# Weight splits and rotations of a decoder layer's front: from VectorE and GpSimd together to VectorE alone

## The chip, the cores and the metric

The kernel runs on one core of one Trainium2 chip. A core has TensorE (matrix products, into PSUM), VectorE, ScalarE and GpSimd (element-wise work), SyncE, which here issues the DMAs, and 16 DMA engines between HBM and SBUF. Each engine works through its own queue in order, and the engines wait for one another on semaphores. The metric is the device time of one execution in microseconds; lower is better.

## The reference

One decoder layer on 256 tokens of width 1024, all in float32. Two attention branches run in parallel on the normed input and are merged through sigmoid gates; a feed-forward part with 32 experts, of which each token uses four, follows; a gated per-layer embedding closes the layer. Cut to what matters here:

```python
proj = rmsnorm(x, g_mix) @ w_in          # q_a, k_a, v_a, c_q, c_kv, k_pe, gate_a, gate_b
q_a = apply_rope(rmsnorm(heads_a(q_a), moba_q_norm))
k_a = apply_rope(rmsnorm(heads_a(k_a), moba_k_norm))
y_a = moba_attention(q_a, k_a, heads_a(v_a))             # 8 heads of 64
q_b = rmsnorm(c_q, mla_q_lat_norm) @ w_uq                # 8 heads of 64 + 32
kv  = rmsnorm(c_kv, mla_kv_lat_norm) @ w_ukv             # k_nope, v_b
k_b = rmsnorm(concat([k_nope, k_pe shared by all heads]), mla_k_norm)
q_b, k_b: apply_rope on the last 32 of 96
y_b = causal_attention(q_b, k_b, v_b)
x = x + (sigmoid(gate_a) * (y_a @ w_branch_a) + sigmoid(gate_b) * (y_b @ w_branch_b)) @ w_out
x = x + routed_experts(rmsnorm(x, g_ffn), ...)           # 32 experts, top 4, clamped SwiGLU
x = x + sigmoid(rmsnorm(x, g_ple) @ w_ple_gate) * (p @ w_ple_proj)
```

`apply_rope` rotates pairs of halves: `[x1*cos - x2*sin, x2*cos + x1*sin]`.

## The kernel before

The program has two parts. The **front**, up to about 212 us, does everything up to the router; the **experts** then stream all 32 experts' weights (2 MB slots, six for each expert) through ten slots of SBUF, four of gate and up weights and two of down weights for each expert. SyncE issues every load in one fixed order (`seq`, `release`); a load is put in the queue where the slot's last reader is programmed, and waits there until that reader is done. Most of the ten slots are used by the front first: for the split weights and activations (`fcr`, `fbr`, `far`), for scratch (`scr0`, `scr1`), for the raw weights (`raw`, later `raw_o`), for the gates. So the front's end hands over most of the ten slots.

**Weight units and their split.** The front's weights are 51 units (lists `KINDS`, `UNITS`): those of the latents, q, k and v projections (four each), sixteen gate units of eight k-tiles by 128 columns, three for the latent up-projections, eight branch units (b) and eight output units (o). Each unit is at most 128x1024 in float32. The products are done in three passes of a reduced format (`three`, L260 to L262): an activation and a weight are each split into a high part, rounded to that format, and a low part, the rest, and high*high, high*low and low*high are summed. `make_unit` makes the two parts: ScalarE casts the unit into `hi` (L216), then `lo = src - hi` (L220) is done by VectorE on the first five eighths of the columns and by GpSimd on the rest; for the o units by VectorE alone. `unit` keeps at most `AHEAD = 3` units made ahead of the one that TensorE uses, in three or four split buffers: the cast of a unit waits until TensorE is done with the unit three before. `fetch` issues the load of a raw unit when the raw buffer's earlier unit has been split.

**Norm and rotation.** `rope_tables` multiplies the norm gains into the cosines and sines (GpSimd, L342 to L356), once for each of four gain vectors (`CA`, `WA` for the first branch, `CB`, `WB` for the second). `moba_norm(i)` squares and sums q or k for the norm, multiplies the swapped halves by `WA` (L412, into `t3`), the straight ones by `CA` (L414, VectorE, into `t5`), adds both (L416, VectorE), and for k scales (L418). The norm of q goes into the softmax's scale. `mla_stats` and `mla_norm` do the same for the second branch: the swapped halves of the 32 rotated columns times `WB` (L521, into `rt2`), the rest by VectorE (L523, L524), and the keys' gain (L526), then scaled per head (L528, L529). The shared key part `kpe` is rotated once (L509 to L512). `rsqrt` is a chain of small VectorE operations (L88 to L97); ScalarE scales the latents with its result (L434, L435).

**Order.** The program is written in the order of the source and scheduled when it is built: a list scheduler sets the order of each engine's queue from an estimate of when operands are there, so operations may stand far from their place in the source. `tc.issue_after(x)` holds the instructions in its block that run on x's engine behind x in that engine's queue; instructions of other engines are not held by it. The rotation tables are so held behind GpSimd's last split made up to there (`last_split[1]`), `x_stats` behind VectorE's (`last_split[0]`), and `mla_norm` behind a masking operation of VectorE (`masked[1]`).

The attention runs in eight rounds (`for j in range(8)`), one pair of heads each: scores on TensorE (L564, L566), masking and maximum on VectorE (L575, L579), exponentials on ScalarE (L581), reciprocal and scaling on VectorE (L583, L585), transposes of the probabilities on TensorE (L594), copies on ScalarE (L596), values on TensorE (L606, L607). Gate units are put between these steps to keep TensorE at work.

Of the kernel before, what the change touches and what calls it, by code (L numbers as in the profile page):

```python
# [27 lines left out]
ALU = mybir.AluOpType  # L28
# [22 lines left out]
UNITS = [(kind, n) for kind, c, n in KINDS for _ in range(c)]  # L51
# [3 lines left out]
FIRST_O = len(UNITS) - 8  # L55
# [10 lines left out]
def hybrid_layer(ctx, tc, x, p, b_down, w_ple_gate, w_ple_proj, bgu3, xt, tabs, wpre, wgu, wdn, out):  # L66
    nc = tc.nc
    V, A, G, T = nc.vector, nc.scalar, nc.gpsimd, nc.tensor
# [138 lines left out]
            load(t, wpre[:, U_OFF[n]:U_OFF[n + 1]])  # L207
            sent_units[0] += 1

    taken, raw_o, last_split = {}, [], [None, None]  # L210

    def make_unit(n):
        src = raw_of(n)[1]
        taken[split_of(n)] = n
        hi, lo = (split[split_of(n)][:, u, 0:UNITS[n][1]] for u in range(2))
        A.copy(hi, src)  # L216
        c = UNITS[n][1] * 5 // 8 if n < FIRST_O else UNITS[n][1]
        for e, a, b in ((V, 0, c), (G, c, UNITS[n][1])):
            if b > a:
                o = e.tensor_tensor(lo[:, a:b], src[:, a:b], hi[:, a:b], op=ALU.subtract)  # L220
                last_split[int(a > 0)] = o.ins

    def unit(k):
        n = used[0]
# [151 lines left out]
    project(512, lambda tt, b: A.mul(qk[:, tt, 0:512], b, xrs[0][:, tt:tt + 1]), x_stats)  # L376
    xrs = xrs[0]

    with tc.issue_after(last_split[1]):
        rope_tables()  # L380


    rbw = wk.tile([P, 2, P], F32, name="rbw")
# [3 lines left out]
    b = bank("rbc")  # L387
# [11 lines left out]
    def moba_norm(i):  # L399
        src, t3, t5 = ([t.rearrange("p (h d) -> p h d", h=8) for t in v] for v in (  # L400
            [qk[:, tt, i * 512:(i + 1) * 512] for tt in range(2)], [sq[:, tt * 512:(tt + 1) * 512] for tt in range(2)],
            [lat[:, tt, 512:1024] for tt in range(2)]))
        for tt in range(2):
            A.square(t3[tt], src[tt])
            V.tensor_reduce(hssb[:, i, tt], t3[tt], axis=AX.X, op=ALU.add)
        if i:
            hrs = rsqrt(wk, hssb.rearrange("p i a b -> p (i a b)"), 32, 64, "ha").rearrange("p (i t h) -> p i t h", i=2, t=2)
            V.tensor_scalar_mul(hrs[:, 0], hrs[:, 0], 64.0 ** -0.5)
            qscale[0], hrs = hrs[:, 0], hrs[:, 1]
        for tt in range(2):  # L410
            for u in range(2):
                G.tensor_tensor(t3[tt][:, :, u * 32:u * 32 + 32], src[tt][:, :, 32 - u * 32:64 - u * 32],  # L412
                                WA[i][:, tt:tt + 1, u * 32:u * 32 + 32].broadcast_to([P, 8, 32]), op=ALU.mult)
            V.tensor_tensor(t5[tt], src[tt], CA[i][:, tt:tt + 1].broadcast_to([P, 8, 64]), op=ALU.mult)  # L414
        for tt in range(2):
            V.tensor_tensor(src[tt], t5[tt], t3[tt], op=ALU.add)  # L416
            if i:
                V.tensor_tensor(src[tt], src[tt], hrs[:, tt].unsqueeze(2).broadcast_to([P, 8, 64]), op=ALU.mult)  # L418
# [21 lines left out]
    for tt in range(2):  # L440
        b = bank("latT")
        for i in range(3):
            T.transpose(b[:, i * P:(i + 1) * P], lsq[:, tt, i * P:(i + 1) * P], ident)
        for i in range(3):
            c = slice(i * P, (i + 1) * P)
# [7 lines left out]
    for c0, c1 in ((0, 512), (512, 768)):  # L453
        wh, wl = unit(2)
        for tt in range(2):
            b = bank("uq")
# [5 lines left out]
    for c0 in (0, 512):  # L462
        for tt in range(2):
            b = bank("ukv")
# [25 lines left out]
    q4 = qb[:, :, 0:768].rearrange("p t (h d) -> p t h d", h=8)  # L490
    kf4 = kbf[:, :, 0:768].rearrange("p t (h d) -> p t h d", h=8)
# [22 lines left out]
    def mla_norm():  # L514
# [3 lines left out]
        brs[0] = r  # L518
        for tt in range(2):
            for u in range(2):  # L520
                G.tensor_tensor(rt2[:, :, u * 16:u * 16 + 16], q4[:, tt, :, 80 - u * 16:96 - u * 16],  # L521
                                WB[0][:, tt:tt + 1, u * 16:u * 16 + 16].broadcast_to([P, 8, 16]), op=ALU.mult)
            V.tensor_tensor(q4[:, tt], q4[:, tt], CB[0][:, tt:tt + 1].broadcast_to([P, 8, 96]), op=ALU.mult)  # L523
            V.tensor_tensor(q4[:, tt, :, 64:96], q4[:, tt, :, 64:96], rt2, op=ALU.add)  # L524
            kr = brs[0][:, tt, 8:16].unsqueeze(2)
            G.tensor_tensor(kf4[:, tt, :, 0:64], kv4[:, tt, :, 0:64],  # L526
                            CB[1][:, tt:tt + 1, 0:64].broadcast_to([P, 8, 64]), op=ALU.mult)
            V.tensor_tensor(kf4[:, tt, :, 0:64], kf4[:, tt, :, 0:64], kr.broadcast_to([P, 8, 64]), op=ALU.mult)  # L528
            V.tensor_tensor(kf4[:, tt, :, 64:96], kpr[:, tt, 0:1].broadcast_to([P, 8, 32]),  # L529
# [112 lines left out]
    for ft in range(8):  # L642
        wh, wl = unit(8)
        bs = []
        for i in range(2):
            b = bank("br")
# [511 lines left out]
```

## Time and profile before

| | |
|---|---|
| runs | 1154.72, 1156.03, 1156.2 us; median 1156.03 |
| profiled execution | 1153.93 us, span 1151.9 us |
| busy over the span | TensorE 1077.9 us (94%), VectorE 328.4 (29%), ScalarE 209.5 (18%), GpSimd 79.0 (7%, 82 instructions, all in the front) |
| DMA | 440.15 MB, mean 382 GB/s |

The span is the time from the first to the last instruction of one profiled execution. Engines appear as PE (TensorE), DVE (VectorE), ACT (ScalarE), POOL (GpSimd) and SP or SPq (SyncE and its DMA queue); L220 is line 220 of the kernel. The share of busy time is a mean over stages with different limits, so it does not tell by itself what sets the end. A wait is shown with what ended it, as `[2.78 <-DVE fr L220]`: 2.78 us without work, ended by VectorE's write of tile `fr` at L220. The tile `fr` holds split parts, `lat` and `pre` hold parts of the norms and rotations, `w_g` and `w_d` expert weights.

### The profile page before, as it was taken

How to read it: one execution, taken by the hardware profiler on the slowest of the kernel's cores; microseconds unless marked ns; L12 is line 12 of the kernel's file. 1: busy time of each engine (PE TensorE's matmuls, PEld its weight loads, DVE VectorE, ACT ScalarE, POOL GpSimd, SP SyncE). 2: the span in 40 equal slices, each digit the busy share in tenths (PEclk: the TensorE clock that was granted, in tenths of full speed). 3: DMA queues.
4: the chain of work that ended last, by engine and by line, in shares of the span. 5: the costliest groups of instructions: out<-in, count | busy, mean ns of one | idle time of the engine just before them, and what ended most of it. 6: DMA issues, size and time to landing. Idle time of an engine off the chain costs nothing. (4 is left out here: it accounts for less than half of the span.)

```text
span 1151.9 us, 13101 instructions
## 1 busy us (share of the span) xinstructions
PE 1077.9 (94%) x5446; PEld 524.7 (46%) x5446; DVE 328.4 (29%) x730; ACT 209.5 (18%) x393; POOL 79.0 (7%) x82
## 2 busy tenths in 40 slices
PE   9799999999999999998889999998998989898988
PEld 7688997543434343342333434343433333333336
DVE  5679688321111121111110111120111111111136
ACT  5576753110000000000001000000000000000024
POOL 5752320000000000000000000000000000000000
PEclk9999999999999999999999999998999999999999
DMA  9544569999999999999999999999999999999991
GB/s 369 189 146 147 183 201 356 374 428 431 432 429 432 430 430 431 431 428 414 430 431 431 429 432 430 430 431 427 431 431 432 427 431 431 430 431 431 428 387 42
DMA packets 40079, 440.15 MB, mean 382 GB/s; under 512 B 4432, under 2 KB 5200, under 8 KB 14832
## 3 DMA queue, kind: packets, MB, share of 16 engines
q1 hardware_dynamic: 40016, 439.27, 91.3%
q8 instruction: 44, 0.72, 0.2%
q14 instruction: 19, 0.16, 0.0%
HBM read 438.21 MB, written 1.05 MB: 381 GB/s over the span
## 5 line engine op out<-in xcount | busy, mean ns | idle before, releaser
L861 PE MATMUL g<-w_g,xg 128*64 128x512 f32 x1024 | 294.5, 600 | 22.0 <-DMA w_g<-in_wgu 17.4
L861 PE MATMUL u<-w_g,xg 128*64 128x512 f32 x1024 | 290.9, 595 | 0.0
L885 PE MATMUL y<-w_d,ht 128*64 128x512 f32 x992 | 227.0, 597 | 11.9 <-DMA w_d<-in_wdn 11.9
L861 PEld LDWEIGHTS g<-w_g,xg 128*64 128x64 f32 x1024 | 78.7, 137 | 167.2 <-issue 122.6
L865 DVE TENSOR_SCALAR g<-g 128x512 f32<-128x512 f32 x32 | 22.1, 692 | 462.2 <-PE g L855 462.2
L861 PEld LDWEIGHTS u<-w_g,xg 128*64 128x64 f32 x1024 | 82.5, 138 | 146.7 <-issue 143.9
L885 PEld LDWEIGHTS y<-w_d,ht 128*64 128x64 f32 x992 | 69.1, 136 | 132.3 <-issue 114.7
L867 ACT ACTIVATE th<-g 128x512 f32<-128x512 f32 x32 | 20.2, 632 | 478.7 <-DVE g L865 478.7
L890 DVE COPY ys<-y 64x512 f32<-64x512 f32 x31 | 21.5, 694 | 168.7 <-ACT ys L889 168.7
L895 PE MATMUL acc<-ys,owT 128*128 128x512 f32 x128 | 59.4, 605 | 8.8 <-ACT ys L889 8.8
L889 ACT COPY ys<-y 64x512 f32<-64x512 f32 x31 | 18.0, 580 | 263.2 <-PE y L885 263.2
L895 PEld LDWEIGHTS acc<-ys,owT 128*128 128x128 f32 x128 | 22.9, 189 | 45.3 <-ACT ys L889 21.1
L822 PE MATMUL g<-oh,h_perm 128*128 128x128 f32 x256 | 33.3, 282 | 6.3 <-DVE g L865 6.2
L822 PEld LDWEIGHTS g<-oh,h_perm 128*128 128x128 f32 x256 | 29.9, 191 | 16.9 <-DVE g L865 11.7
L822 PEld LDWEIGHTS u<-oh,h_perm 128*128 128x128 f32 x256 | 29.8, 192 | 8.1 <-issue 8.1
L220 POOL TENSOR_TENSOR fr<-raw_x,fr 128x384 fp32r<-128x384 f32 (+1 forms) x21 | 29.2, 1399 | 47.8 <-ACT fr L216 47.8
L822 PE MATMUL u<-oh,h_perm 128*128 128x128 f32 x256 | 32.2, 279 | 0.0
L261 PE MATMUL proj<-fr,fr 128*128 128x512 f32 (+1 forms) x64 | 26.2, 409 | 5.6 <-DVE fr L220 5.4
L260 PE MATMUL gate<-fr,fr 128*128 128x256 f32 x104 | 30.5, 293 | 0.0
L262 PE MATMUL gate<-fr,fr 128*128 128x256 f32 x104 | 29.6, 285 | 0.7 <-DVE fr L220 0.7
L834 DVE TENSOR_SCALAR ow<-oh,whalf 128x128 f32<-128x128 f32 x64 | 14.0, 283 | 54.6 <-PE owT L847 54.6
L261 PE MATMUL gate<-fr,fr 128*128 128x256 f32 x104 | 29.4, 283 | 0.0
(320 smaller groups left out, 1161.2 us busy)
## 6 DMA issues: line engine op xcount, KB each, us to landing
w_g<-in_wgu SPq DMA_DIRECT2D x124, 2048.0 KB, 31.9
w_d<-in_wdn SPq DMA_DIRECT2D x62, 2048.0 KB, 32.6
raw_x<-in_wpre SPq DMA_DIRECT2D x29, 512.0 KB, 3.7
w_g<-in_wgu SPq DMA_DIRECT2D x8, 1024.0 KB, 27.9
raw<-in_wpre SPq DMA_DIRECT2D x12, 512.0 KB, 8.3
w_ple<-in_w_ple_gate SPq DMA_DIRECT2D x8, 512.0 KB, 10.0
raw_o<-in_wpre SPq DMA_DIRECT2D x4, 512.0 KB, 5.0
w_d<-in_wdn SPq DMA_DIRECT2D x2, 1024.0 KB, 25.8
```

The costliest lines, as they stand in the source:

```text
L220: o = e.tensor_tensor(lo[:, a:b], src[:, a:b], hi[:, a:b], op=ALU.subtract)
L260: T.matmul(o, lh, rh, start=first, stop=False)
L261: T.matmul(o, lh, rl, start=False, stop=False)
L262: T.matmul(o, ll, rh, start=False, stop=last)
L822: T.matmul(b[:, k * P:(k + 1) * P], h_perm[:, tt, (half * 4 + k) * P:(half * 4 + k + 1) * P], oh[:, tt], start=(tt == 0), stop=(tt == 1))
L861: T.matmul(gu[i][half * CAP:(half + 1) * CAP], xg[:, k], wv_, start=(k == 0), stop=False)
L865: V.tensor_scalar_min(g, gu[0], 7.0)
L867: A.activation(th, g, AF.Tanh, scale=0.851)
L885: T.matmul(y[g * CAP:(g + 1) * CAP], ht[:, f % 4, (f // 4) * CAP:(f // 4 + 1) * CAP], w[:, dh * 512:(dh + 1) * 512], start=(f == 0), stop= ...
L889: A.copy(ys[0:CAP, odd], y[0:CAP])
L890: V.tensor_copy(ys[CAP:P, 1 - odd], y[CAP:P])
L895: T.matmul(acc[tt][dh], owT[:, dh, tok(tt)], ys[:, dh], start=first, stop=last)
```

## The change

Three things. In `make_unit` the low part of every unit is one VectorE instruction over all its columns; GpSimd has no share. The rotation tables are no longer held behind a split, as there is none on GpSimd. And three sorts of multiplications move from GpSimd to VectorE: the swapped halves in `moba_norm` (eight of 128x256), those in `mla_norm` (four of 128x128), and the keys' gain in `mla_norm` (two of 128x512). GpSimd keeps the tables, the router weights' gain `w_r` and the shared key. Since `mla_norm` is called inside `tc.issue_after(masked[1])`, and `masked[1]` is on VectorE, the moved multiplications of `mla_norm` now fall under that hold.

```diff
-    taken, raw_o, last_split = {}, [], [None, None]
+    taken, raw_o, last_split = {}, [], [None]
 
     def make_unit(n):
         src = raw_of(n)[1]
         taken[split_of(n)] = n
         hi, lo = (split[split_of(n)][:, u, 0:UNITS[n][1]] for u in range(2))
         A.copy(hi, src)
-        c = UNITS[n][1] * 5 // 8 if n < FIRST_O else UNITS[n][1]
-        for e, a, b in ((V, 0, c), (G, c, UNITS[n][1])):
-            if b > a:
-                o = e.tensor_tensor(lo[:, a:b], src[:, a:b], hi[:, a:b], op=ALU.subtract)
-                last_split[int(a > 0)] = o.ins
+        last_split[0] = V.tensor_tensor(lo, src, hi, op=ALU.subtract).ins
...
-    with tc.issue_after(last_split[1]):
-        rope_tables()
+    rope_tables()
...
         for tt in range(2):
             for u in range(2):
-                G.tensor_tensor(t3[tt][:, :, u * 32:u * 32 + 32], src[tt][:, :, 32 - u * 32:64 - u * 32],
+                V.tensor_tensor(t3[tt][:, :, u * 32:u * 32 + 32], src[tt][:, :, 32 - u * 32:64 - u * 32],
                                 WA[i][:, tt:tt + 1, u * 32:u * 32 + 32].broadcast_to([P, 8, 32]), op=ALU.mult)
...
             for u in range(2):
-                G.tensor_tensor(rt2[:, :, u * 16:u * 16 + 16], q4[:, tt, :, 80 - u * 16:96 - u * 16],
+                V.tensor_tensor(rt2[:, :, u * 16:u * 16 + 16], q4[:, tt, :, 80 - u * 16:96 - u * 16],
                                 WB[0][:, tt:tt + 1, u * 16:u * 16 + 16].broadcast_to([P, 8, 16]), op=ALU.mult)
...
-            G.tensor_tensor(kf4[:, tt, :, 0:64], kv4[:, tt, :, 0:64],
+            V.tensor_tensor(kf4[:, tt, :, 0:64], kv4[:, tt, :, 0:64],
                             CB[1][:, tt:tt + 1, 0:64].broadcast_to([P, 8, 64]), op=ALU.mult)
```

## Rows read from the trace of the kernel before

**Rows 1.** Stretches: span, then each engine's busy time, PEclk, DMA share, GB/s.

```profile
210.00:220.00 10.00, 10.00 (x57) 4.66 (x57) 2.27 (x7) 0.00 (x0) 0.00 (x0) 1.00 0.72 270
220.00:1114.00 894.00, 841.85 (x3986) 327.33 (x3982) 146.78 (x279) 67.17 (x117) 0.00 (x0) 1.00 1.01 429
```

**Rows 2.** The chain that ended last, one late piece: start, duration, what.

```profile
1093.42 20.77 DMA w_d<-in_wdn
```

**Rows 3.** Timeline of SyncE's queue at the first release by expert 0.

```profile
215.93 0.33 SPq L80 DMA_DIRECT2D w_g<-in_wgu  x1
```

**Rows 4.** Timeline, 38 to 49 us, around the first long wait of a projection.

```profile
38.06 1.49 DVE L416 TENSOR_TENSOR qk<-lat,pre 128x512 f32<-128x512 f32 x1 [2.73 <-POOL pre L412]
...
40.88 0.79 DVE L416 TENSOR_TENSOR qk<-lat,pre 128x512 f32<-128x512 f32 x1 [1.33 <-POOL pre L412]
...
41.82 0.99 POOL L220 TENSOR_TENSOR fr<-raw_x,fr 128x384 fp32r<-128x384 f32 x1
41.92 0.92 DVE L90 TENSOR_SCALAR lat_s<-lat_m 128x4 int32<-128x4 int32 x1
...
44.43 0.50 PE L261 MATMUL proj<-fr,fr 128*128 128x512 f32 x1 [2.78 <-DVE fr L220]
...
45.46 0.51 ACT L434 ACTIVATE lat<-lat,lat_r 128x256 f32<-128x256 f32 x1 [8.35 <-DVE lat_r L97]
...
47.92 0.83 DVE L220 TENSOR_TENSOR fr<-raw_x,fr 128x640 fp32r<-128x640 f32 x1 [2.50 <-ACT fr L216]
...
48.64 0.28 PE L260 MATMUL gate<-fr,fr 128*128 128x256 f32 x1
```

**Rows 5.** Timeline, 50 to 58 us, around the second long wait.

```profile
50.23 1.51 DVE L414 TENSOR_TENSOR lat<-qk,pre 128x512 f32<-128x512 f32 x1
...
54.27 1.47 DVE L416 TENSOR_TENSOR qk<-lat,pre 128x512 f32<-128x512 f32 x1 [1.34 <-POOL pre L412]
...
55.66 1.61 DVE L220 TENSOR_TENSOR fr<-raw,fr 128x640 fp32r<-128x640 f32 x1
...
57.33 0.50 PE L261 MATMUL proj<-fr,fr 128*128 128x512 f32 x1 [2.66 <-DVE fr L220]
```

**Rows 6.** Timeline, 83 to 92 us, the first round of the attention.

```profile
83.57 2.10 DVE L507 TENSOR_SCALAR bss<-bss,kps 128x8 f32<-128x8 f32 x2
...
87.21 1.01 DVE L579 SCALAR_TENSOR_TENSOR mx<-mx,ha_r 128x2 f32<-128x2 f32 x1
...
90.38 0.61 PE L594 MATMUL PT<-cst,pr 128*128 128x128 f32 x3 [1.49 <-DVE pr L585]
...
90.67 0.82 DVE L220 TENSOR_TENSOR fr<-raw_x,fr 128x640 fp32r<-128x640 f32 x1
...
91.83 0.30 PE L594 MATMUL PT<-cst,pr 128*128 128x128 f32 x1 [0.84 <-DVE pr L585]
```

**Rows 7.** Waits up to 216 us: total us, times, longest us.

```profile
PE rbc L389 <- DVE rbw L386: 0.7, 1, 0.7
...
PE gate L262 <- DVE fr L220: 0.7, 1, 0.7
```

**Rows 8.** Stretches of the attention, columns as in rows 1.

```profile
82.00:92.00 10.00, 6.92 (x57) 5.86 (x56) 9.91 (x36) 8.80 (x24) 4.66 (x5) 1.00 0.72 262
...
122.00:150.00 28.00, 27.59 (x222) 24.84 (x221) 17.65 (x68) 20.52 (x53) 9.91 (x6) 1.00 0.50 170
```

**Rows 9.** The stretch behind the first long wait, columns as in rows 1.

```profile
45.19:48.60 3.41, 3.41 (x9) 2.63 (x8) 0.88 (x3) 3.14 (x6) 0.64 (x1) 0.50 0.49 154
```

**Rows 10.** GpSimd's groups by form: busy us, mean ns, idle before and releaser.

```profile
L220 POOL TENSOR_TENSOR fr<-raw_x,fr 128x384 fp32r<-128x384 f32 x20 | 28.2, 1417 | 47.8 <-ACT fr L216 47.8
...
L412 POOL TENSOR_TENSOR pre<-qk,pre 128x256 f32<-128x256 f32 x8 | 7.1, 902 | 2.9 <-DVE hssb L405 2.9
```

**Rows 11.** VectorE's groups by form, up to 212 us.

```profile
L373 DVE TENSOR_TENSOR sg<-gate,rbc 128x256 f32<-128x256 f32 x16 | 6.7, 417 | 2.4 <-PE gate L262 2.4
...
L220 DVE TENSOR_TENSOR fr<-raw_o,fr 128x1024 fp32r<-128x1024 f32 x4 | 4.9, 1218 | 0.0
```

## Prediction

> **What bounds the kernel now.** I read the late part first. From 220 to 1114 us the DMA share is 1.01 at 429 GB/s, while TensorE has 842 of 894 us busy [rows 1]; the chain that ended last runs back through the last expert weights [rows 2]. So the end is the end of the weight stream plus a fixed tail, and the stream is set by when it starts. Its loads wait for slots that the front still uses: the queue issues the first load behind expert 0 at 215.93, after TensorE has read expert 0's first slices [rows 3]. Between 210 and 220 the DMA share is 0.72, 2.8 us of nothing [rows 1]. Whatever brings TensorE to expert 0 earlier brings the stream, and the end, earlier by as much, since the loads of 176 to 198 are released by the same front.
>
> Second, the front, where the change lies: in which stretches TensorE stands, and who ends its waits. Nearly all of it lies in four places. A projection waits 2.78 us until 44.43, and the next one 2.66 us until 57.33, both for VectorE's split at L220 [rows 4, 5]. The transposes of the probabilities wait 1.49 and 0.84 us at 90.38 and 91.83, for VectorE's scaling [rows 6]. Two waits of 0.7 us are for VectorE as well [rows 7]. In 82 to 92 us TensorE is busy 6.9 us of 10 and VectorE 9.9; later, in 122 to 150 us, TensorE 27.6 and VectorE 17.7 of 28 [rows 8]. And a wait has a tail: at 45.19, just behind the first, the granted clock is 0.50, the lower level of 1.2 GHz, for 3.41 us; a second such stretch, as long, follows the second (one of the two stands in [rows 9]). At half speed 3.41 us lose 1.7 us.
>
> Third, what VectorE was doing before those two splits. Before the first it stood 2.73 and 1.33 us for GpSimd's L412 [rows 4]; before the second 1.34 us for the same [rows 5].
>
> **The change part by part.** GpSimd gives up 57 of its 82 instructions: 43 shares of splits (38 of 384 columns, mean 1.42 us for the largest group), eight L412 at 0.90 us, four L521, two L526 [rows 10]. What it keeps, the rotation tables, `w_r` and the shared key, already stands in its queue.
>
> VectorE takes all of it over. A whole split of 1024 columns takes 1.22 us where GpSimd had no share [rows 11]; one of 640 takes 0.83 when nothing stood in front of it [rows 4]. So a split grows by 0.39 us, 38 times, 14.8 us; the four of 832 and the one of 512 columns add 1.5 by the same slope. The rotations are not to be seen on VectorE. The nearest row for 128x256 is L373, 0.42 us [rows 11]: eight L412 are 3.4 us, four L521 of half that size at most 1.7, two L526 of twice that size 1.7. Their strided and broadcast operands could make them dearer; the upper bound is GpSimd's 0.90 us for 256 columns [rows 10], by which they are 14.4 instead of 6.8 us, and the lower is nothing, if they fall into time in which VectorE stood. I take 6.8 us, since L416 adds 512 columns in 0.79 us at 40.88 [rows 4], about twice L373. Together VectorE gains 23 us of work over a front of 212 us.
>
> What it gets back is the time in which it is held. Its instructions stand still while GpSimd works: L90, on four elements, starts at 41.92 and takes 0.92 us, to the end of the GpSimd split that began at 41.82; L416 takes 1.49 us at 38.06 and 0.79 at 40.88 [rows 4]; the split at 55.66 takes 1.61 us instead of 0.83 [rows 5]; two L507 on eight elements take 2.10 us together and the L579 at 87.21, on two, 1.01 [rows 6]. So the engines worked in turns, and a split was whole when GpSimd's share was, after 1.4 us in the mean. With one engine it is whole after 1.22 us, but its first 640 columns come 0.39 us later.
>
> Now each wait of TensorE, by what changes in VectorE's queue in front of the split that it waits for.
>
> *First wait, 41.65 to 44.43.* Away go 4.06 us of standing for L412, 0.70 at the first L416 and 0.75 at L90 (0.92 less an assumed 0.17), 5.5 us. In come four L412, 1.7 us, and two larger splits, 0.8. Net, the split ends 3.0 us earlier, at about 41.4, and the wait is gone. What is late next: ScalarE holds a weight cast behind L434, which starts only at 45.46, when VectorE has the root of the latents, after 8.35 us of waiting; that cast feeds the split at 47.92, and that split the gate unit that TensorE starts at 48.64 [rows 4]. This chain also moves by 3.0 us, so the split starts at 44.9 and, 1.22 us long, ends at 46.1. TensorE needed 4.2 us from 44.43 to the gate unit, 1.7 of it lost to the clock; from 41.65 it is there at 44.2. It now starts the unit at 46.1, 2.5 us earlier than before, behind a new wait of 1.9 us. I assume that the clock stays up behind it: the waits of 1.49 and 0.84 us at 90.38 and 91.83, 2.3 us in 2.9, left it at 1.00 [rows 6, 8].
>
> *Second wait, 54.67 to 57.33.* Away go 1.34 us of standing, 0.8 at L414 (1.51 us at 50.23), 0.7 at L416 and 0.8 at the split itself [rows 5], 3.6 us; in come two L412 and three larger splits, 2.0 us. The split is 1.6 us earlier against its surroundings, a wait of 1.0 us stays, and the slow clock goes with its 1.7 us: 3.3 us.
>
> *Third wait, 88.9 to 91.8.* L507 and L579 were held for some 1.8 and 0.8 us; against that one split in front grows by 0.39. The first piece, 1.49 us, goes and half of the second: 1.9 us.
>
> *Small waits.* The two of 0.7 us stand behind VectorE work of which GpSimd held the parts in the same way; I take 1.3 of 1.4 us.
>
> The sum is 2.5 + 3.3 + 1.9 + 1.3 = 9.0 us. From it I take 1 us for first halves of splits that now come 0.39 us later where TensorE is close behind, as at the very first unit: 8.0 us. No DMA is added or moved past another in SyncE's queue; refills of the raw weights, which waited for both engines' shares of a split, are released by VectorE's alone. The rotation tables lose their place behind GpSimd's last split and run as soon as their input has landed; there they hold VectorE as they did before, some microseconds sooner.
>
> Against the profiled execution, 1151.9 us of span and 1153.93 in all, this gives 1145.9. That execution is 2.1 us below the median of the runs shown; from the median, 1156.03, it is 1148.0.
>
> From 82 to 92 us VectorE is 9.9 of 10 us busy, and by the order of before at least two larger splits and two L526, 2.5 us, would come into it or just behind; the held time of [rows 6], 2.6 us, pays for that. A rule of the Trainium skill speaks against the change here: Perfetto Trace Analysis, section Optimizing Scalar/DVE Operations, would move work off a saturated VectorE, to GpSimd if need be, and it warns in the same place that the two share a read port, so that this might not help. By its first half the stretch would be 2.5 us longer and the third wait's 1.9 us would not come, 1152.4 in all; by its warning, which the held L507 bears out, 1148.
>
> **The rivals.** *The clock falls again.* The new wait at the gate unit, 1.9 us, lies between those that left the clock up and 2.66 us, which did not. If it and the rest of the second wait still end in 3.4 us at half speed each, 3.4 us of the gain are gone: 1151.4. For it speaks that these waits are worked out from differences; against it, that both are shorter than the two that were followed by the slow clock. 22 in 100.
>
> *The stream does not follow.* If the loads issued between 176 and 198 us hung on something that does not move, an earlier start of expert 0 could fill only the 2.8 us hole at 210 to 220: 1153 to 1156. For it: the stream is what ends last. Against it: in that stretch the loads wait for slots that TensorE and VectorE work in, and both come earlier. 9 in 100.
>
> *The splits get in the way of the softmax, and it is slower.* Place: VectorE's queue in the eight rounds of head pairs from 82 to 150 us. At 90.67 a split of 0.82 us already stands in front of a scaling for which TensorE waits [rows 6]. Two whole splits there would be 2.44 us, 1.62 more in each round, 13 us in eight; the third wait would stay too, so with 6.1 us left of the gain the end is 6.9 us later, at 1163. It decides from 0.8 us of new waits per round, at which nothing is left. For it: VectorE is 9.9 of 10 us busy when the rounds begin. Against it: from 122 to 150 us it has 10 us free [rows 8]. 13 in 100.
>
> **How the numbers follow.** The forecast has the other 56 in 100 and a range of its own of 1145 to 1151. The low end of the whole range takes all these waits away and both slow stretches: 2.78 + 2.66 + 1.49 + 0.84 + 1.4 + 3.4 is 12.6 us, 1143. At the high end the rotations' upper bound, 7.6 us dearer and wholly in TensorE's way, gives 1155.6; with the second rival that is 1156, which leaves out the slower one and little else. What a measurement of this kernel can tell from no change is 0.2%, 2.3 us. Faster: the forecast, the first rival and the edge of the second, 80. The same: the rest of the second and the mild part of the third, 8. Slower: 12.
>
> **What would show it.** Right: GpSimd busy with its tables and the key alone, L416 without idle time before it, L90, L507 and L579 at 0.2 us, splits at 1.22 us; no wait of TensorE over 2 us before 80 us and no half clock there; the load that was issued at 215.93 now near 208, and the stream from there on as before. Wrong: long waits of the projections for L220 with VectorE busy throughout, half-clock stretches that stay, or transposes of the probabilities that wait in each round. The prediction fails most easily by the order of VectorE's queue, which is made anew when the program is built and which I took from before.

## The result, and the profile after

The changed kernel takes 1141.75 us (median of 1139.96, 1141.3, 1142.2, 1142.97), the kernel before 1155.38 beside it (four runs): a ratio of 0.9882, 95% interval 0.9867 to 0.9897, 13.6 us faster. The forecast was 1148.0, that is 8.0 us faster, with a range of 1143 to 1156: the direction was right, the gain too small by 5.6 us. The profiled executions differ by as much, 1153.93 and 1139.96, with spans of 1151.9 and 1138.3.

Lines after the change: the split is L217 (was L220), L407 was L412, L411 was L416, L429 was L434, L580 and L589 were L585 and L594, L256 to L258 were L260 to L262. First, stretches of the changed kernel, columns as in [rows 1]:

```profile
40.00:44.00 4.00, 4.00 (x19) 3.34 (x18) 3.73 (x12) 2.48 (x9) 1.72 (x3) 1.00 0.58 177
44.00:50.00 6.00, 6.00 (x39) 5.43 (x38) 4.88 (x8) 4.98 (x9) 0.00 (x0) 1.00 0.52 131
50.00:56.00 6.00, 6.00 (x28) 4.96 (x27) 5.97 (x16) 2.58 (x3) 0.00 (x0) 1.00 0.73 227
72.00:82.00 10.00, 7.77 (x64) 6.71 (x63) 9.01 (x40) 10.00 (x27) 0.00 (x0) 1.00 0.77 270
82.00:92.00 10.00, 10.00 (x87) 9.23 (x86) 9.66 (x43) 6.03 (x16) 0.00 (x0) 1.00 0.31 100
...
197.00:207.00 10.00, 10.00 (x56) 4.37 (x57) 1.78 (x4) 0.00 (x0) 0.00 (x0) 1.00 0.89 346
207.00:1100.00 893.00, 843.13 (x3980) 328.89 (x3978) 146.88 (x279) 67.03 (x117) 0.00 (x0) 0.99 1.01 429
```

From 40 to 56 us TensorE is busy throughout, and the granted clock is 1.00 in every stretch of the front; the half clock of [rows 9] is gone. The stream of expert weights runs as it did in [rows 1], 1.01 at 429 GB/s. It starts earlier, as SyncE's queue in the timeline shows; this row answers to [rows 3]:

```profile
202.38 0.33 SPq L80 DMA_DIRECT2D w_g<-in_wgu  x1
```

That is 13.55 us earlier than 215.93, and TensorE's first product of expert 0 moves from 212.23 to 198.69, 13.54 us earlier. The end moves by the same 13.6. So the first link of the argument held: what the front gives up, the end gives up.

Next the timeline around the place of the first long wait, which answers to [rows 4]:

```profile
35.66 1.42 DVE L407 TENSOR_TENSOR pre<-qk,pre 128x256 f32<-128x256 f32 x4
...
36.30 1.06 ACT L216 CAST fr<-raw_x 128x1024 fp32r<-128x1024 f32 x1
...
37.00 0.69 DVE L411 TENSOR_TENSOR qk<-lat,pre 128x512 f32<-128x512 f32 x1
...
37.60 1.22 DVE L217 TENSOR_TENSOR fr<-raw_x,fr 128x1024 fp32r<-128x1024 f32 x1
...
39.02 1.05 ACT L216 CAST fr<-raw_x 128x1024 fp32r<-128x1024 f32 x1 [1.66 <-PE proj L258]
...
40.85 1.21 DVE L217 TENSOR_TENSOR fr<-raw_x,fr 128x1024 fp32r<-128x1024 f32 x1
...
41.54 0.39 PE L256 MATMUL proj<-fr,fr 128*128 128x512 f32 x1
...
43.08 0.51 ACT L429 ACTIVATE lat<-lat,lat_r 128x256 f32<-128x256 f32 x1 [0.29 <-DVE lat_r L97]
...
44.26 0.28 PE L256 MATMUL gate<-fr,fr 128*128 128x256 f32 x1
```

The four rotations L407 take 1.42 us in all and L411 follows without idle time. Unit 12, for which TensorE waited until 44.43 before, is cast at 36.30 and split at 37.60, some 2.7 us before TensorE is there. Unit 13, the gate unit, is cast at 39.02, ahead of L429; before, its cast stood behind that scaling of the latents. Its split is done at 42.06, and TensorE goes into it at 44.26 without a wait, where the prediction had a new wait of 1.9 us.

One wait of [rows 6] has stayed (timeline):

```profile
79.18 0.61 PE L589 MATMUL PT<-cst,pr 128*128 128x128 f32 x3 [0.24 <-DVE pr L580]
81.03 0.30 PE L589 MATMUL PT<-cst,pr 128*128 128x128 f32 x1 [1.25 <-DVE pr L580]
```

And the groups of VectorE in the front by form, as in [rows 10, 11]:

```profile
L217 DVE TENSOR_TENSOR fr<-raw,fr 128x1024 fp32r<-128x1024 f32 x12 | 14.7, 1225 | 7.2 <-ACT fr L216 7.2
...
L407 DVE TENSOR_TENSOR pre<-qk,pre 128x256 f32<-128x256 f32 x8 | 3.1, 420 | 0.0
L411 DVE TENSOR_TENSOR qk<-lat,pre 128x512 f32<-128x512 f32 x4 | 2.8, 691 | 0.0
L521 DVE TENSOR_TENSOR kbf<-scr,pre 128x512 f32<-128x512 f32 x2 | 1.4, 688 | 0.0
```

A whole split takes 1.22 us, a rotation of 128x256 0.42, and L411 0.69 where it took 1.49 and 0.79 in [rows 4]. VectorE's busy time up to expert 0 is 156.9 us, against 157.6 before. It took on 16.3 us in the splits, by the prediction's working, and 5.6 us of rotations (3.1, 1.4, and 1.1 for four of 0.29), and is no longer busy than it was. So, by this estimate, about 22 us of what the trace of before counts as VectorE's work was standing still for GpSimd.

### The profile page after: what moved, and what is told of

It is laid out like the page before. It is cut to its first block, busy times and chain, and to the rows that moved or that the text cites. A ratio compares the mean times of both kernels' runs of the same rounds, so it can differ in the third digit from the quotient of the medians.

```text
span 1138.3 us, 13004 instructions
## 1 busy us (share of the span) xinstructions
PE 1073.8 (94%) x5446; PEld 523.4 (46%) x5446; DVE 327.8 (29%) x744; ACT 209.0 (18%) x393; POOL 10.2 (1%) x25
## 3 DMA queue, kind: packets, MB, share of 16 engines
HBM read 438.21 MB, written 1.05 MB: 386 GB/s over the span
## 5 line engine op out<-in xcount | busy, mean ns | idle before, releaser
L856 PE MATMUL g<-w_g,xg 128*64 128x512 f32 x1024 | 297.9, 601 | 21.4 <-DMA w_g<-in_wgu 17.0
L856 PE MATMUL u<-w_g,xg 128*64 128x512 f32 x1024 | 295.3, 597 | 0.0
L256 PE MATMUL gate<-fr,fr 128*128 128x256 f32 x104 | 30.5, 294 | 0.0
L217 DVE TENSOR_TENSOR fr<-raw_x,fr 128x1024 fp32r<-128x1024 f32 (+1 forms) x24 | 28.9, 1205 | 5.5 <-ACT fr L216 5.1
L258 PE MATMUL gate<-fr,fr 128*128 128x256 f32 x104 | 29.5, 284 | 0.0
L216 ACT CAST fr<-raw_x 128x1024 fp32r<-128x1024 f32 (+1 forms) x24 | 24.9, 1036 | 18.1 <-PE br L257 5.5
```

Of the source, the lines that this page charges most:

```text
L217: last_split[0] = V.tensor_tensor(lo, src, hi, op=ALU.subtract).ins
L256: T.matmul(o, lh, rh, start=first, stop=False)
L258: T.matmul(o, ll, rh, start=False, stop=last)
L856: T.matmul(gu[i][half * CAP:(half + 1) * CAP], xg[:, k], wv_, start=(k == 0), stop=False)
```

## Experiments

The kernels were timed in four groups, each in turn with the kernel before on one chip; "earlier" is one less the ratio, times 1155 us, and kernels of different groups are compared by it. Beside it stands how much earlier than 212.23 TensorE reaches expert 0 in the profiled execution.

| kernel | time, us | ratio (95%) | earlier, us | expert 0 earlier, us |
|---|---|---|---|---|
| the change | 1141.75 | 0.9882 (0.9867 to 0.9897) | 13.6 | 13.5 |
| splits alone | 1144.43 | 0.9922 (0.9909 to 0.9935) | 9.0 | 12.4 |
| rotations alone | 1144.37 | 0.9917 (0.9904 to 0.9930) | 9.6 | 8.8 |
| hold of the tables alone | 1153.45 | 0.9990 (0.9981 to 0.9999) | 1.2 | -0.9 |
| change + idle work of 384 columns | 1153.89 | 0.9993 (0.9975 to 1.0011) | 0.8 | 0.9 |
| change + idle work of 64 columns | 1141.89 | 0.9881 (0.9863 to 0.9900) | 13.7 | 12.6 |
| change, cast of unit 13 held | 1142.43 | 0.9889 (0.9871 to 0.9906) | 12.8 | 12.0 |
| before + fill in the waits | 1153.00 | 0.9985 (0.9970 to 0.9999) | 1.7 | 1.9 |
| change, unit 12 late | 1147.24 | 0.9930 (0.9910 to 0.9950) | 8.1 | 8.1 |
| the same + fill | 1144.28 | 0.9901 (0.9882 to 0.9919) | 11.4 | 9.5 |
| change, splits made twice | 1144.22 | 0.9905 (0.9887 to 0.9923) | 11.0 | 11.6 |
| change, GpSimd empty | 1142.47 | 0.9888 (0.9869 to 0.9906) | 12.9 | 14.3 |
| change + three orders | 1138.72 | 0.9858 (0.9838 to 0.9878) | 16.4 | 15.5 |

The two last columns agree within 3.4 us, and within 2.1 in all rows but one. The fourth column is one execution, which need not be a middling one: that of the hold of the tables took 1156.58 us, the longest of its eleven runs. Within the profiled executions span and arrival agree within 2.4 us. So the end follows TensorE's arrival at expert 0, up to some 2 us, mostly lost again behind it, that I did not trace.

**Half of the change at a time.** The splits alone, with the rotations back on GpSimd:

```diff
-                V.tensor_tensor(t3[tt][:, :, u * 32:u * 32 + 32], ...
+                G.tensor_tensor(t3[tt][:, :, u * 32:u * 32 + 32], ...
-                V.tensor_tensor(rt2[:, :, u * 16:u * 16 + 16], ...
+                G.tensor_tensor(rt2[:, :, u * 16:u * 16 + 16], ...
-            V.tensor_tensor(kf4[:, tt, :, 0:64], kv4[:, tt, :, 0:64],
+            G.tensor_tensor(kf4[:, tt, :, 0:64], kv4[:, tt, :, 0:64],
```

> The changed kernel with the rotations back on GpSimd: splits whole on VectorE, tables without their hold, the eight rotations of L407, the four of L516 and the two of L521 on GpSimd. Theory (the engines work in turns, so what counts is how much of GpSimd's time goes): the splits were 58 of the 69 us that left GpSimd, so this alone gives 9 to 11 of the 13.6 us, 1144 to 1146; VectorE still stands before L411 for about 2 us, and a first wait of up to 1 us stays. Rival (the time came from VectorE's standing for L412, 2.73, 1.33 and 1.34 us in front of the two long waits): those waits stay, 2 to 4 us are gained, 1151 to 1153.

The rotations alone are the reverse of these three lines in the kernel before:

> The kernel before with the rotations alone on VectorE; the splits stay shared 5/8 to 3/8, the tables keep their hold. Theory (turns, by GpSimd's time): 11 of 69 us leave GpSimd and the standing of VectorE for L412 with them; the first wait falls from 2.78 to 0.5 to 1 us and the second to about 2, so 4 to 5 us are gained, 1150 to 1151. Rival (standing for L412 is all of it): both long waits and both stretches at half clock go, 9 us or more, 1146.

Each alone is worth 9 to 10 us by the time (12.4 and 8.8 us by the arrival). So the theory's numbers held for the first kernel and failed for the second: by GpSimd's busy time the rotations should have brought 4 to 5. There the rival's numbers held, 9 us or more and no half clock. The rival's claim, that standing for L412 is all of it, is not settled by this pair: with the splits alone VectorE's waits for the rotations fall too, from 6.1 to 2.0 us, as GpSimd has no splits in front of them. How much of the gain is standing for results and how much being held these two kernels do not separate. The two do not add up, 18.6 against 13.6, because they shorten the same two waits. With the splits alone nothing is left of the first and 0.62 us of the second; with the rotations alone the first is gone, and 0.88 us is left, at a later unit of the same projection. Neither kernel shows a half clock anywhere in the front behind its start, so the tails of both waits go with either half. And with the rotations alone the predicted new wait does come (timeline of that kernel, TensorE):

```profile
45.71 0.39 PE L260 MATMUL gate<-fr,fr 128*128 128x256 f32 x1 [0.85 <-ACT fr L216]
46.57 0.39 PE L262 MATMUL gate<-fr,fr 128*128 128x256 f32 x1 [0.36 <-DVE fr L220]
```

There the gate unit waits 1.21 us, first for ScalarE's cast and then for the split.

**The place of the tables.** One line of the change in the kernel before:

```diff
-    with tc.issue_after(last_split[1]):
-        rope_tables()
+    rope_tables()
```

> The kernel before with one line undone: the rotation tables no longer held behind GpSimd's last split. Theory: no change, within 1 us of 1155; the tables run some 3 us sooner and hold VectorE there instead. Rival (the place of the tables freed GpSimd for the first rotations): L412 starts earlier and the first wait shrinks by 2 us or more, 1152 or less.

The first wait did shrink, to 0.85 us, and 1.08 us at the gate unit came in its place; the second stayed (timeline, TensorE, and two stretches):

```profile
43.20 0.50 PE L261 MATMUL proj<-fr,fr 128*128 128x512 f32 x1 [0.85 <-DVE fr L220]
46.72 0.39 PE L260 MATMUL gate<-fr,fr 128*128 128x256 f32 x1 [0.73 <-ACT fr L216]
47.58 0.39 PE L262 MATMUL gate<-fr,fr 128*128 128x256 f32 x1 [0.35 <-DVE fr L220]
56.09 0.50 PE L261 MATMUL proj<-fr,fr 128*128 128x512 f32 x1 [2.64 <-DVE fr L220]
```

```profile
56.09:59.50 3.41, 3.41 (x9) 2.69 (x10) 2.72 (x5) 1.35 (x2) 2.46 (x3) 0.56 0.64 165
...
90.60:94.10 3.50, 3.41 (x16) 3.44 (x17) 3.50 (x14) 2.87 (x8) 0.55 (x1) 0.51 0.50 150
200.00:204.00 4.00, 4.00 (x22) 3.75 (x22) 2.39 (x17) 2.35 (x3) 0.00 (x0) 0.50 1.03 416
```

The clock stayed up behind the first and fell at 90 instead, behind the transposes' waits; the half clock among the router's products lasted from 200 to 206.8, twice as long as before. The time moved by 1.2 us: about the theory's number, but with the rival's change at the first wait, paid back later.

**GpSimd at work beside VectorE, with nothing waiting for it.**

```diff
         last_split[0] = V.tensor_tensor(lo, src, hi, op=ALU.subtract).ins
+        if n < FIRST_O:
+            G.tensor_tensor(idle, hi[:, 0:384], hi[:, 0:384], op=ALU.subtract)
```

> The changed kernel, and beside each split of the front's first 43 units GpSimd subtracts 384 columns of the upper half from themselves into a tile that nothing reads. Nothing waits for its result. Theory (the two engines hold each other up): splits grow from 1.22 to some 1.8 to 2.5 us in the mean, VectorE's short instructions to 0.9 us where they meet, and the end comes 6 us later or more, 1148 to 1156. Rival (only the waits for GpSimd's results cost time): splits stay at 1.22 us and the time at 1141 to 1143.

All but 0.8 us of the gain is gone, though no instruction reads `idle`. This separates the two readings: it is not the waits for GpSimd's results alone, its running costs. One dependency was overlooked: the subtraction reads `hi`, so ScalarE's casts into the same buffers waited for GpSimd four times (0.27 and 1.37 us at 41.63 and 44.05, 0.93 at 58.28, 1.38 at 124.85). By the trace none of TensorE's waits hangs on these: behind each such cast its split stood in VectorE's queue anyway, or TensorE had other work. The timeline of that kernel, VectorE's chain for the first norm:

```profile
28.41 4.40 POOL L220 TENSOR_TENSOR idle<-fr 128x384 f32<-128x384 f32 x4
28.50 1.82 DVE L218 TENSOR_TENSOR fr<-raw,fr 128x1024 fp32r<-128x1024 f32 x1 [0.81 <-ACT fr L217]
30.25 0.78 DVE L95 TENSOR_TENSOR x_t<-x_r 128x2 f32<-128x2 f32 x1
31.06 0.16 DVE L96 SCALAR_TENSOR_TENSOR x_t<-x_t,x_m 128x2 f32<-128x2 f32 x1
31.25 0.67 DVE L97 SCALAR_TENSOR_TENSOR x_r<-x_t,x_r 128x2 f32<-128x2 f32 x1
...
33.40 0.38 PE L387 MATMUL rbc<-cst,rbw 128*128 128x128 f32 x1 [3.35 <-DVE rbw L384]
```

The rbc product spreads the root of the first norm over the partitions for the gate units. Behind its wait TensorE is at half clock again (stretch):

```profile
33.80:37.20 3.40, 3.40 (x18) 3.40 (x18) 3.40 (x6) 2.56 (x5) 0.00 (x0) 0.51 1.02 398
```

A split that starts 0.09 us after GpSimd takes 1.82 us instead of 1.22, and instructions on two elements take 0.67 to 0.78 instead of 0.16; TensorE waits 3.35 us for the end of that chain, against 1.06 in the changed kernel. This wait and its slow stretch are some 4 of the 12.6 us that expert 0 comes later, in a place where the kernel before lost little: four subtractions had piled up in GpSimd's queue behind the tables. So the run shows that GpSimd's work alone costs as much as the gain, not that it costs it in the places of before. My number for the splits was wrong: their mean is 1.30 to 1.36 us, as it is mostly VectorE that starts first; then GpSimd stands, and its 384 columns take 1.80 us instead of 0.83. The Trainium skill, SBUF — State Buffer, section Who interferes with whom, says that a VectorE instruction with two inputs in SBUF contends with a GpSimd instruction that reads SBUF, for ports that the two engines share; the one that starts first has them for its whole instruction, and the other stands. The trace agrees, with 0.78 us for L95, a product of two elements.

With 64 columns instead of 384 in the same place:

> The changed kernel, and beside each split of the front's first 43 units GpSimd subtracts 64 columns (0.31 us in the rows of the tables) into a tile that nothing reads, instead of 384. Theory (the engines exclude each other for as long as GpSimd works): 13 us of its time instead of 62, so a fifth of the 12 us, some 2.5 us later than the changed kernel, 1144. Rival (each handover costs, whatever the length): most of the 12 us, 1150 or more. Third (short instructions fit into VectorE's free time): 1142.

No cost, the third case. The groups of that kernel by form:

```profile
L220 POOL TENSOR_TENSOR idle<-fr 128x64 f32<-128x64 f32 x37 | 38.2, 1033 | 86.8 <-ACT fr L217 86.5
```

```profile
L218 DVE TENSOR_TENSOR fr<-raw_x,fr 128x1024 fp32r<-128x1024 f32 x22 | 27.0, 1227 | 5.9 <-ACT fr L217 5.5
```

GpSimd is now busy 44.8 us with these instructions, three quarters of what it was with six times the columns, and the splits have their 1.22 us: the shortest of them takes 0.29 us, so most of a mean of 1033 ns is GpSimd's standing for VectorE. So GpSimd's busy time, by which I had sized the two halves above, is no measure of what it costs VectorE.

**The cast of unit 13.** Back behind the scaling of the latents, as before the change:

```diff
+            with tc.issue_after(lat_done[-1]) if m == 13 else ExitStack():
-            make_unit(m)
+                make_unit(m)
```

Here `lat_done` is that scaling's last instruction, and unit 13 is made after it in the source.

> The changed kernel with one order put back as it was before the change: ScalarE's cast of unit 13, a gate unit, held behind the scaling of the latents by their root. Theory (the prediction's new wait was absent because this cast now ran ahead of that scaling): the scaling ends near 44.3, the cast near 45.4, the split near 46.6, TensorE is there at 44.3 and waits 2.0 to 2.5 us; the end is that much later, 1144, or 1146 if the granted clock falls to its lower level behind the wait. Rival (the first wait was mis-sized for another reason, such as the clock): the cast finds another gap, no wait over 0.5 us, 1141 to 1143.

The rival's numbers, a wait under 0.5 us and a time of 1142.43, but for another reason. The timeline of ScalarE and that of TensorE:

```profile
42.58 0.39 ACT L432 ACTIVATE lat<-lat,lat_r 128x128 f32<-128x128 f32 x1
42.88 1.03 ACT L217 CAST fr<-raw_x 128x1024 fp32r<-128x1024 f32 x1
```

```profile
43.96 0.39 PE L258 MATMUL gate<-fr,fr 128*128 128x256 f32 x1
44.19 0.28 PE L259 MATMUL gate<-fr,fr 128*128 128x256 f32 x1
44.91 0.73 PE L258 MATMUL proj<-fr,fr 128*128 128x512 f32 x2 [0.45 <-ACT fr L217]
45.48 0.28 PE L260 MATMUL gate<-fr,fr 128*128 128x256 f32 x1
```

The cast begins at 42.88, 1.4 us earlier than expected: the root is done sooner, as no split stands in its chain in this order. And TensorE starts the gate unit before the split: the first two of three products need only the cast half, and two products of unit 14 were put in between. From the gate unit to the transposes of the latents TensorE takes 14.61 us instead of 13.79, so the order costs 0.8 us here, not 1.9. At expert 0 it is 1.6 us, as the wait for `xs`, the new residual in front of the router, is 1.4 us instead of 0.4. The time does not tell it from the changed kernel.

**The clock.** First a fill in the kernel before:

```diff
+            if used[0] - 1 in (12, 15):
+                with tc.issue_after(mm[0]):
+                    keep_warm(22)
```

`mm[0]` is the last product issued; `keep_warm` multiplies a constant tile, and the projections' products are held behind it in the order of the source.

> The kernel before, with 22 small products of a constant tile (128x256, some 0.11 us each, 2.4 us in all) put into TensorE's queue in front of unit 12 and of unit 15, so that TensorE works through most of its two long waits. Theory (a long wait costs its length and then 1.7 us more of half clock): both stretches at half clock go and the waits stay, 3.4 us earlier, 1151. Rival (after an undisturbed clock TensorE merely waits longer for VectorE's next splits): the stretches go but the time moves by less than 1.5 us, 1153 to 1155.

The rival's mechanism; by the time, 1.7 us earlier, its bound of 1.5 was just missed, and the interval, 0.1 to 3.5 us, does not exclude the theory's 3.4. Both stretches go, and TensorE, now earlier, waits 1.79 us at 61.57 for VectorE; half clock follows there, and again at 90 (stretches, columns as above):

```profile
61.57:65.00 3.43, 3.43 (x10) 2.67 (x11) 3.09 (x11) 0.82 (x2) 1.41 (x2) 0.61 0.54 153
...
90.00:94.00 4.00, 3.71 (x21) 3.74 (x22) 3.97 (x15) 3.07 (x9) 0.85 (x1) 0.62 0.48 135
```

Where VectorE is late, part of what the clock gives is lost again in the next wait for it. In the changed kernel VectorE has time to spare, so a wait made there shows the tail by itself. Unit 12's split was put behind unit 14's; its lower half is then formed from the weights that have landed in its buffer since, so the k projection is not the reference's, at the same work:

```diff
+        if n == 12:
+            late.append((lo, src, hi))
+            return
         last_split[0] = V.tensor_tensor(lo, src, hi, op=ALU.subtract).ins
+        if n == 14:
+            with tc.issue_after(last_split[0]):
+                late.append(V.tensor_tensor(late[0][0], late[0][1], late[0][2], op=ALU.subtract).ins)
...
-    lrs = rsqrt(wk, lss.rearrange("p a b -> p (a b)"), 4, 256, "lat")
+    with tc.issue_after(late[1]):
+      lrs = rsqrt(wk, lss.rearrange("p a b -> p (a b)"), 4, 256, "lat")
```

Beside this, TensorE's products of units 9 to 17 are held in the order of the source.

> The changed kernel with one long wait made on purpose: the split of unit 12 is put behind that of unit 14 in VectorE's queue (and the latents' root behind it), and TensorE keeps its order of units, so that it waits for unit 12 from about 41.5 to 45.4 us, some 3.8 us, in the place where the kernel before waited 2.78. Theory (a long wait costs its length and, behind it, a stretch at half clock of 3.4 us that loses 1.7): 5.5 us later than the changed kernel, 1147. Rival (only the wait costs): 3.8 us, 1145.5. Third (VectorE behind by more than the wait): later than 1148.

> The same kernel with the same late split of unit 12, and 36 small products of a constant tile (0.11 us each, 3.9 us) in TensorE's queue through that wait. VectorE's and TensorE's orders are otherwise the same. Theory: no half clock behind it, so 1.7 us earlier than with the bare wait, 1145.5. Rival (the clock costs nothing here, because TensorE waits again for the next splits): the same time as with the bare wait, within 0.5 us.

The bare wait is 3.30 us, and the stretch behind it is at half clock; with the fill it is not (stretches of the first and of the second kernel):

```profile
44.98:48.39 3.41, 3.41 (x8) 2.76 (x9) 1.83 (x12) 1.17 (x4) 0.00 (x0) 0.51 0.41 138
```

```profile
45.06:48.50 3.44, 3.44 (x21) 2.96 (x19) 1.74 (x11) 1.32 (x4) 0.00 (x0) 1.00 0.40 141
```

Eight products of 512 columns fit into the first stretch; into the second all twelve of unit 12 and nine of the next. TensorE enters the gate unit at 49.21 and at 47.88; at expert 0 the 1.3 us are still there, 204.09 against 202.74. The fill itself ended 0.1 us later than the bare wait and had one more product behind it, 0.2 us, so the tail is 1.6 us. The whole wait costs 5.4 us at expert 0 and 5.5 in the time: theory. The fill's gain is larger in the time, some 3 us where the theory had 1.7, but the six runs of the bare wait spread over 3.8 us; I go by the arrival.

**Room in the rounds of the attention.**

```diff
         last_split[0] = V.tensor_tensor(lo, src, hi, op=ALU.subtract).ins
+        if 23 <= n < 35:
+            last_split[0] = V.tensor_tensor(lo, src, hi, op=ALU.subtract).ins
```

> The changed kernel with the splits of the twelve gate units of the rounds of head pairs (units 23 to 34) made twice, the same into the same tile: VectorE has 14.7 us more work between 75 and 145 us and TensorE waits for the second. Theory (VectorE keeps free time there, some 12 us between 82 and 150, and units are made three ahead): part is hidden, 3 to 7 us later, 1145 to 1149. Rival (the splits stand in front of the softmax's scaling in each round): all of it shows, 13 us or more, 1155 and later. Third case, all hidden: 1142.

It is 2.7 us later by the ratios, just under the theory's range, for 14.7 us of work. VectorE's busy time up to expert 0 is 169.0 us. With the idle work of 384 columns it was 170.5, and that cost 12.8: what counts is not how much VectorE is busy but where. From 92 to 112 us it is full, and TensorE, busy 19.03 us there against 19.23 in the changed kernel, hardly notices:

```profile
92.00:112.00 20.00, 19.03 (x159) 17.18 (x158) 20.00 (x54) 12.90 (x28) 0.00 (x0) 1.00 0.34 98
```

**GpSimd empty.** The tables, `w_r` and `kpr` to VectorE as well (`G.` to `V.` in those lines):

> The changed kernel with the rest of GpSimd's work, the rotation tables, the scaling of the router's weights and the shared key (25 instructions, 10.2 us on GpSimd), on VectorE as well, GpSimd empty. Theory (VectorE is held by the tables from 19 to 27 us, where its splits take 1.23 to 1.30 and the root that the rbc product waits for is late): some 0.5 to 1 us earlier, 1141. Rival (VectorE is now too full between 19 and 30 us): rbc and the first gate unit come later, 1 us or more lost, 1143 and later.

TensorE is at expert 0 0.8 us earlier, at 197.91, the time is the same: the rest of GpSimd's work costs nothing that these runs can tell.

**Three orders more.** On the changed kernel, at the waits that are left:

```diff
-    gate_unit()
+    gate_unit(make_rbc)
...
+            with tc.issue_after(scaled[3]) if m == 25 else ExitStack():
-            make_unit(m)
+                make_unit(m)
...
-    weights()
+    with tc.issue_after(posm_ins):
+        weights()
```

`make_rbc` holds the two products for rbc and the copy behind them, and runs behind the gate unit's own products; `scaled[3]` is the last scaling of the first softmax round, `posm_ins` VectorE's `posm`, for which the first gather waits.

> The changed kernel with three more edits of order, at the three longest waits that are left in its front: the small product for rbc behind the gate unit's products instead of ahead of them (1.06 us), the split of unit 25 behind the scalings of the first softmax round (up to 0.9 of 1.25 us), VectorE's work on the routing weights behind posm (1.25 us before the first gather). If the end follows TensorE's arrival at expert 0 one to one: 3 us less than the changed kernel, 1138 to 1139. If the gains are eaten by the next wait in each place: 1140.5 to 1142.

1138.72 us, the lowest of all kernels here. TensorE is at expert 0 at 196.70, 2.0 us earlier than in the changed kernel; the wait of 1.06 us is gone, 0.53 is left of 1.25 in front of the first gather and 0.44 of 1.49 at the transposes, while the wait for `xs` grew from 0.42 to 1.07. The intervals of the two ratios overlap, so the time alone does not settle it against the changed kernel; the arrival, of one execution each, speaks for it.

## Why the prediction was too small

Term by term, by when TensorE enters a stage before and after:

| term | predicted, us | measured, us | from |
|---|---|---|---|
| first wait | 2.5 | 4.7 | rbc product to gate unit: 29.59 to 48.64, 29.93 to 44.26 |
| second wait | 3.3 | 4.6 | gate unit to transposes of the latents: to 67.07, to 58.05 |
| third wait | 1.9 | 0.8 | scores to gate unit behind the transposes: 84.00 to 92.34, 74.03 to 81.55 |
| small waits | 1.3 | 1.0 | next gate unit, to the scores |
| first halves later | -1.0 | -0.3 | rbc product 29.59, 29.93 |
| from 92 us to expert 0 | 0 | 2.8 | 92.34 to 212.23, 81.55 to 198.69 |
| sum | 8.0 | 13.5 | |

Two steps failed most: the new wait of 1.9 us that the first wait's term put in, and the stretch from 92 us to expert 0, which the sum left at nothing without a reason.

**The first wait.** Its 3.0 us of net earlier work, and a wait that goes, were right; the new wait of 1.9 us at the gate unit was not there. It was reckoned with ScalarE's queue as it stood before, with the cast of unit 13 behind the scaling of the latents. In the kernel that was built the cast stands ahead of it. That is the failure the prediction had named, the order of the queues; but putting that order back cost only 0.8 us. The rest was my working: the root was taken 1.0 us too late (the split at 44.9, where it is at 43.94 in that kernel), and I let TensorE wait for the whole split, though two of its three products need only the cast. The wait itself is real: 1.21 us with the rotations alone, 1.08 with the tables alone.

**The second wait** was to keep 1.0 us; it went altogether, with its tail. This is the same step, VectorE's queue taken from before: in the splits-only kernel 0.62 us stays.

The wait for the rbc product, half of the small waits, did not go but grew from 0.71 to 1.06 us; the term for the first halves, meant for such places, covers it.

**The tails** were sized rightly, 1.7 us each at half clock; the purpose-made wait measured 1.6. Both were counted, and 3.4 us of the gain is theirs.

**From 92 us to expert 0.** "Nearly all of it lies in four places" was a wrong reading: it left out some 4 of 13 us of TensorE's waits, among them 0.99 us for VectorE's `xs` and 0.51 at 112.17, and a third stretch at half clock, at 202 us among the router's small products. Timeline of TensorE before and after:

```profile
198.25 1.26 PE L671 MATMUL hT<-cst,xs 128*128 128x128 f32 x8 [0.99 <-DVE xs L694]
...
202.32 4.61 PE L281 MATMUL warm<-warm 128*128 128x256 bf16 x26
```

```profile
185.50 1.25 PE L666 MATMUL hT<-cst,xs 128*128 128x128 f32 x8 [0.42 <-DVE xs L689]
...
189.24 3.00 PE L277 MATMUL warm<-warm 128*128 128x256 bf16 x26
...
194.95 2.02 PE L817 MATMUL g<-oh,h_perm 128*128 128x128 f32 x16 [1.25 <-issue]
```

Of the 2.8 us, 0.8 lie between the transposes of `xs` (198.25, 185.50) and expert 0: the half clock had cost the 26 small products 1.6 us, but a new wait of 1.25 us in front of the first gather takes most of it back. The shorter wait for `xs` is 0.6, the wait at 112.17, which is gone, 0.5. The remaining 0.9 us are in pieces that I did not take apart.

**The third wait** was oversized. A split of 1.22 us stands at 79.47 in front of a scaling for which TensorE waits 1.25 us; the prediction gave this mechanism its place under the slower rival and did not charge it to this term. Holding that one split back, in the last kernel, took 1.05 of the 1.49 us that are left of 2.33.

**The rivals.** The clock did not fall again: behind the start, no wait of more than 1.25 us was left in the front. The stream followed, to 0.1 us. The splits do get in the softmax's way once, in the first round, but not in each: even made twice they cost 2.7 us, not 13.

**The cause.** That the engines work in turns was read rightly from L90 and L507, and the idle work shows it by itself: 12.8 us back with no result of GpSimd used. How the gain divides between being held and standing for L412 stays open. Of the rule weighed in the prediction (the Trainium skill, Perfetto Trace Analysis, section Optimizing Scalar/DVE Operations) the warning held and the advice did not: in the first round VectorE was busy 9.91 of 10 us before (82 to 92) and 9.01 after it had taken the work (72 to 82). What was sized wrongly is how far VectorE's queue would run ahead once nothing held it. I moved each of its instructions by the differences just in front of a wait; in fact units were split 2 to 3 us before TensorE needed them, so that the long waits of the projections vanished whole, where I had left remainders.

## What to carry to other kernels

When a change frees the engine that several waits hang on, do not reckon each wait by its own few instructions and the old order of the queues: work out where the freed engine's queue would stand, and if it is ahead of its reader, take the whole wait and what follows it. List every wait and every slow stretch up to the end of the part that sets the time, the small ones too, before a stretch is put at nothing. Two halves of a change that shorten the same wait are not worth their sum; run each alone. And before pricing an engine by its busy time, ask how much of that time it stood: VectorE took 22 us of work and was not busier, GpSimd did a sixth of the columns in three quarters of the time.

## What the runs showed of the hardware

- GpSimd's subtraction of 384 columns takes 0.83 us at its shortest and 1.80 us when it starts 0.1 us after a VectorE split (idle work of 384 columns). Even an instruction of VectorE on two or four elements that meets GpSimd's takes 0.67 to 0.92 us instead of 0.16 or 0.17.
- A TensorE wait of 3.30 us was followed by 3.41 us at a granted clock of 0.51, the lower level of 1.2 GHz; with small products in place of the wait the clock stayed at 1.00. With the idle work a wait of 3.35 us was followed by the same.
- Half clock also followed a wait of 1.79 us (61.57, before with the fill) and waits of 1.45 and 0.84 us (near 90, in that kernel and in the one without the tables' hold). It did not follow 1.49 and 0.84 us in the kernel before [rows 6, 8].
